# One layer on one Trainium2 core: in the mixer's step list, the query projection moves from third place to just ahead of the query convolution

## The chip, the cores and the metric

The kernel runs on one core of one Trainium2 chip. The metric is device time in microseconds, from three runs of the kernel before: a median of 1311.32 us, the lowest 1310.68, the highest 1312.76. One execution more was taken with the hardware profiler, and all the rows below come from it. In this document PE is the matrix engine (TensorE), DVE is VectorE, ACT is ScalarE, POOL is GpSimd and SP is the engine that issues the loads. Each of them works through its own instructions in their order.

## What is computed

One layer works on 512 latent tokens and 256 context tokens of width 1024, in fp32: a feed-forward block, a mixer, another feed-forward block and a norm. Only the beginning of the mixer matters here. There, one input projection yields the following, each from its own columns of `w_in`:

```python
proj = h_all @ w_in
hg_q, hg_i, hg_g, hg_f_fwd, hg_f_bwd, ml_q, ml_k, ml_v, ml_o, ml_gates = jnp.split(proj, splits, axis=-1)
qk = jax.nn.silu(short_conv(jnp.concatenate([ml_q, ml_k], axis=-1), conv_w, conv_b, n_ctx)).astype(f32)
gates = ml_gates.astype(f32) + ml_gate_b.astype(f32)
i_fwd, f_fwd, i_bwd, f_bwd = jnp.split(gates, 4, axis=-1)
logf_dir = jax.nn.log_sigmoid(jnp.concatenate([f_fwd, seg_reverse(f_bwd, n_ctx)], axis=0))
```

`short_conv` is a depthwise convolution, 3x3 over the latent grid and 3 taps over the context. From the gates come running sums and running maxima over the tokens, in both directions; they weigh the keys and values of the mLSTM heads.

## The kernel before

All products are made from operands that are split into a high and a low part, so each product takes three matmuls (high by high, high by low, low by high). For a weight tile, `load_w` (line 274) has SP load 128x1024 numbers (512 KB) into a buffer `wraw`, ACT round them into `whi`, and DVE subtract to get `wlo`. There are **two** buffers `wraw`, so a load waits until the DVE subtraction that last read its buffer is over. `whi` and `wlo` have three buffers each. The mixer's own pool has eight buffers named `d6`, which hold many things in turn, and eight PSUM banks: five named `mm` and three named `aux`.

The mixer is a list of steps, `MIXER` (line 37). Each name is a step and a number; the loop at line 1181 calls them in that order, and a scheduler orders the instructions of each engine when the kernel is built, mostly along that list, by its own estimates of time. So the order on each engine is fixed before the kernel runs. The steps that matter:

- `iv1`: a half of the HGRN2 values, 144 matmuls of 256 columns into three banks (`proj_v`).
- `ck0`, `ck1`: the convolution of the two halves of the keys (`ml_conv_ctx`, `ml_conv_lat`): POOL clears a padded `d6` buffer, ACT copies the projection into it, DVE does 3 taps on 256 columns and 9 taps on 512, ACT a sigmoid, DVE a product.
- `mq0`: the query projection, two weight tiles, 48 matmuls of 512 columns. Its first tile's two parts lie in `d6` buffers (`spare`, line 1154), the second's in `whi` and `wlo`.
- `vals0`: a half of the mLSTM values together with the gates (`proj_vg`, line 715), 144 matmuls of 272 columns: 256 of values and 16 of gates. The two weight tiles lie in four `d6` buffers of 272 columns. Their last 16 columns come from another small load (`in_wg`) and are split by themselves, two small instructions each on ACT and DVE. Each of the six token tiles' gates is copied by ACT to a buffer.
- `rows0`: the gate rows (`ml_rows`, line 901): PE turns the gates over (6 transposes); then a chain of some 30 instructions on ACT and DVE, on 36 or 4 rows by 768: absolute value, exponential, logarithm, running sums and maxima, exponentials.
- `cols0` (`ml_cols`, line 980): PE turns the results of the gate rows over (10 transposes). It waits for `rows0`.
- `cq1`, `cq0`: the convolution of the two halves of the queries. `iv0`, `vals1`: the other halves of the values, 144 matmuls each. `pair0` and the rest of the list: the heads themselves. `pair0` begins on PE with 6 transposes of the keys.

Of the kernel before, what the change touches and what calls it, by code (L numbers as in the profile page):

```python
# [23 lines left out]
for _n, _w in (("nw", 32), ("bmod", 72), ("gb", 1), ("cw", 36), ("cbias", 4), ("hgw", 4), ("mlw", 4)):  # L24
# [9 lines left out]

MIXER = ("iv1 ck0 mq0 vals0 ck1 rows0 cq1 cols0 iv0 vals1 cq0 pair0 pair0 pair0 pair1 prep0 prep0 fin4 scan0 "
         "pair1 scan0 prep1 state0 pair1 prep1 state0 prep2 scan1 scan1 state1 prep2 state1 prep3 scan2 fin0 "
         "fin5 scan2 prep3 gate0 fin1 state2 gate5 state2 scan3 gate1 scan3 gate7 state3 fin2 gate2 gate6 "
         "state3 gate4 fin3 gate3").split()  # L40
# [58 lines left out]
class Builder:  # L99
# [1043 lines left out]
    def mixer(self, st, start):  # L1143
# [36 lines left out]
        going = {}  # L1180
        for x in MIXER:
            if x not in going:
# [392 lines left out]
```

## Time and profile before

| what | us |
|---|---|
| median of three runs | 1311.32 |
| the profiled execution, its own time | 1312.59 |
| span of the profiled execution, first to last instruction | 1310.8 |
| PE busy in the span | 1286.0 (98%) |
| DVE busy | 1012.4 (77%) |
| ACT busy | 578.0 (44%) |
| POOL busy | 56.5 (4%) |
| the chain that ended last: share on PE | 94% |

The mixer's list begins at about 584 us of the span and ends at about 905 us. The views used below are the page of the profile (its chain that ended last), the busy time of the engines by stretches, the timelines of single engines (start, duration, engine, line, operation, destination and sources, shape, count; in square brackets the idle time ahead and what ended it), and the summary of the tile `wraw`. Line 56 stands for all instructions, since a helper records them, so rows are told apart by their tiles and shapes. The clock column is the TensorE clock that was granted, as a share of 2.4 GHz; 0.50 is the lower level of 1.2 GHz.

### The profile page before, as it was taken

What the parts mean: (1) busy time and instruction counts of PE and PEld (TensorE: products, weight loads), DVE (VectorE), ACT (ScalarE), POOL (GpSimd) and SP (SyncE); (2) the same over time, 40 slices, a digit from 0 to 9 for tenths busy, and PEclk for the clock granted to TensorE, in tenths of its full rate; (3) what the DMA queues carried; (4) which work ended last, traced back from release to release, by engine and by line L of the source; (5) the groups of instructions that cost most, each with busy time, mean ns of one, the idle gap of its engine ahead of it and who ended that gap; (6) DMA issues with size and microseconds to landing.
All of it is one profiled execution on the core that took longest, in us unless ns stands there. A gap on an engine that the chain in (4) does not pass through costs nothing.

```text
span 1310.8 us, 20560 instructions
## 1 busy us (share of the span) xinstructions
PE 1286.0 (98%) x8210; PEld 1179.8 (90%) x8210; DVE 1012.4 (77%) x1620; ACT 578.0 (44%) x992; POOL 56.5 (4%) x81
## 2 busy tenths in 40 slices
PE   8999999999999999999989999999999999999997
PEld 4689999999998888999978798889998999999996
DVE  6995778777789888767676867986588788888766
ACT  5553444444442222383457343444473444444434
POOL 2000000000000000110100000000000000000001
PEclk8999999999999999999989999999999999999998
DMA  9224443344686866413041101114233222233301
GB/s 347 106 93 151 140 146 125 133 140 145 214 289 228 271 209 195 145 47 117 3 145 49 65 34 49 65 50 175 83 107 136 97 97 97 102 108 104 106 17 65
DMA packets 48803, 163.60 MB, mean 125 GB/s; under 512 B 5554, under 2 KB 10034, under 8 KB 48708
## 3 DMA queue, kind: packets, MB, share of 16 engines
q1 hardware_dynamic: 46308, 150.50, 33.4%
q0 software_dynamic: 2400, 11.80, 2.8%
q8 instruction: 64, 1.05, 0.3%
q14 instruction: 31, 0.25, 0.1%
HBM read 149.39 MB, written 12.89 MB: 124 GB/s over the span
## 4 chain that ended last, share of the span: by engine, by line
PE 94%; DVE 2%; ACT 2%; issue 1%; POOL 0%; DMA 0%; POOLq 0%; DVEq 0%
PE mm L56 72%; PE aux L56 21%; DVE mod_scr L56 1%; ACT xh L56 1%; DVE x L56 0%; ACT nm_y L56 0%; ACT x L56 0%; DVE wlo L56 0%; ACT nm_t L56 0%; ACT whi L56 0%; DVE xl L56 0%; POOL rms_acc L56 0%; DVE s L56 0%; DVE nm_x L56 0%; DMA four<-in_cc 0%
## 5 line engine op out<-in xcount | busy, mean ns | idle before, releaser
L56 PE MATMUL mm<-xh,whi 128*128 128x256 f32 (+2 forms) x1072 | 345.7, 323 | 1.2 <-ACT xh L56 1.2
L56 PE MATMUL mm<-xh,wlo 128*128 128x256 f32 (+2 forms) x1072 | 342.4, 320 | 0.8 <-DVE wlo L56 0.8
L56 PE MATMUL mm<-xl,whi 128*128 128x256 f32 (+2 forms) x1000 | 323.4, 324 | 2.9 <-DVE xl L56 2.9
L56 PEld LDWEIGHTS mm<-xh,whi 128*128 128x128 f32 x1072 | 203.3, 190 | 14.3 <-ACT xh L56 1.9
L56 PEld LDWEIGHTS mm<-xh,wlo 128*128 128x128 f32 x1072 | 203.4, 190 | 10.8 <-DVE wlo L56 1.0
L56 PE MATMUL mm<-six,whi 128*128 128x384 f32 (+1 forms) x752 | 209.3, 359 | 0.0
L56 PEld LDWEIGHTS mm<-xl,whi 128*128 128x128 f32 x1000 | 189.8, 190 | 14.7 <-DVE xl L56 4.3
L56 ACT ACTIVATE whi<-wraw 128x1024 fp32r<-128x1024 f32 x100 | 105.9, 1062 | 170.4 <-PE aux L56 91.5
L56 PEld LDWEIGHTS mm<-six,whi 128*128 128x128 f32 x752 | 135.7, 188 | 10.0
L56 PE MATMUL mm<-six,wlo 128*128 128x384 f32 (+1 forms) x376 | 134.4, 357 | 0.0
L56 DVE TENSOR_TENSOR wlo<-wraw,whi 128x1024 fp32r<-128x1024 f32 x100 | 121.7, 1219 | 10.5 <-ACT whi L56 10.4
L56 DVE CUSTOM_DVE_ANT_0 mod_scr<-wm,cb 128x1024 bf16<-128x1024 f32 x84 | 105.4, 1255 | 2.8 <-DMA wm<-in_w_mod 2.6
L56 PEld LDWEIGHTS mm<-six,wlo 128*128 128x128 f32 x376 | 70.6, 188 | 6.5
L56 DVE SCALAR_TENSOR_TENSOR x<-mm,mod_l,x 128x256 f32<-128x256 f32 (+1 forms) x88 | 51.9, 601 | 18.3 <-PE mm L56 17.5
L56 DVE TENSOR_TENSOR wlo<-four,whi 128x1024 fp32r<-128x1024 f32 x37 | 45.3, 1225 | 26.7 <-ACT whi L56 26.7
L56 PE MATMUL aux<-ah,w2hi 128*128 128x512 f32 x160 | 64.0, 400 | 0.0
L56 ACT ACTIVATE whi<-four 128x1024 fp32r<-128x1024 f32 x37 | 39.2, 1061 | 56.1 <-PE mm L56 46.1
L56 PE MATMUL aux<-al,w2hi 128*128 128x512 f32 x160 | 63.1, 394 | 0.0
L56 DVE SCALAR_TENSOR_TENSOR x<-aux,mod_l,x 128x512 f32<-128x512 f32 x80 | 58.9, 745 | 5.2 <-PE aux L56 5.2
L56 PE MATMUL aux<-ah,w2lo 128*128 128x512 f32 x160 | 62.4, 390 | 0.0
L56 PE MATMUL mm<-tl,whi 128*128 128x256 f32 x216 | 61.0, 283 | 0.0
L56 PE MATMUL aux<-six,whi 128*128 128x256 f32 x320 | 59.0, 282 | 0.0
(336 smaller groups left out, 2553.8 us busy)
## 6 DMA issues: line engine op xcount, KB each, us to landing
wraw<-in_f1w SPq DMA_DIRECT2D x62, 512.0 KB, 3.9
wm<-in_w_mod SPq DMA_DIRECT2D x58, 512.0 KB, 4.0
wraw<-in_f2w SPq DMA_DIRECT2D x44, 512.0 KB, 3.4
wraw<-in_wi SPq DMA_DIRECT2D x32, 512.0 KB, 3.3
w2raw<-in_f2w SPq DMA_DIRECT2D x22, 512.0 KB, 4.2
four<-h SPq DMA_DIRECT2D x22, 384.0 KB, 4.7
h<-x POOLq DMA_DIRECT2D x18, 384.0 KB, 3.0
wraw<-in_wo SPq DMA_DIRECT2D x8, 512.0 KB, 4.0
```

The source lines that it names most:

```text
L56: r = f(*a, **kw)
```

## The change

One word moves in the list:

```diff
-MIXER = ("iv1 ck0 mq0 vals0 ck1 rows0 cq1 cols0 iv0 vals1 cq0 pair0 pair0 pair0 pair1 prep0 prep0 fin4 scan0 "
+MIXER = ("iv1 ck0 vals0 ck1 rows0 mq0 cq1 cols0 iv0 vals1 cq0 pair0 pair0 pair0 pair1 prep0 prep0 fin4 scan0 "
```

The scheduler then puts the instructions of all engines in another order from this place to the third head. What is done stays the same. Three places follow. The numbers behind a name tell buffers of one name apart.

**DVE, from the first split for the moved projection to the small splits of the gate columns** (`w2_5547` is the first key half's latent convolution, `w2_5809` and `w2_5818` or `w2_5747` and `w2_5756` the second's). Before; `d6_5562` and `wlo_5593` are the low parts of `mq0`, `d6_5630` and `d6_5638` those of `vals0`, `wlo_5932` of `iv0`:

```order
L56 TENSOR_TENSOR d6_5562<-wraw_5560,d6_5561 128x1024
L56 TENSOR_SCALAR w2_5547<-d6_5544,cst_110 128x512
L56 SCALAR_TENSOR_TENSOR w2_5547<-d6_5544,cst_110,w2_5547 128x512
L56 TENSOR_TENSOR wlo_5593<-wraw_5591,whi_5592 128x1024
L56 SCALAR_TENSOR_TENSOR w2_5547<-d6_5544,cst_110,w2_5547 128x512 x3
L56 TENSOR_TENSOR d6_5630<-wraw_5628,d6_5629 128x4x256
L56 SCALAR_TENSOR_TENSOR w2_5547<-d6_5544,cst_110,w2_5547 128x512 x4
L56 TENSOR_TENSOR d6_5638<-wraw_5636,d6_5637 128x4x256
L56 SCALAR_TENSOR_TENSOR d6_5315<-w2_5547,w2_5557 128x512
L56 TENSOR_TENSOR wlo_5932<-wraw_5930,whi_5931 128x1024
L56 TENSOR_TENSOR d6_5630<-w2_5626,d6_5629 128x4x16
L56 TENSOR_TENSOR d6_5638<-w2_5626,d6_5637 128x4x16
```

Now; `d6_5576` is a low part of `vals0`, `wlo_5864` the second one of `mq0`:

```order
L56 TENSOR_TENSOR d6_5576<-wraw_5574,d6_5575 128x4x256
L56 SCALAR_TENSOR_TENSOR w2_5547<-d6_5544,cst_110,w2_5547 128x512 x6
L56 TENSOR_TENSOR wlo_5864<-wraw_5862,whi_5863 128x1024
L56 SCALAR_TENSOR_TENSOR w2_5547<-d6_5544,cst_110,w2_5547 128x512
L56 SCALAR_TENSOR_TENSOR d6_5315<-w2_5547,w2_5557 128x512
L56 TENSOR_SCALAR w2_5747<-d6_5744,cst_110 128x256
L56 TENSOR_SCALAR w2_5756<-d6_5753,cst_110 128x512
L56 SCALAR_TENSOR_TENSOR w2_5747<-d6_5744,cst_110,w2_5747 128x256
L56 SCALAR_TENSOR_TENSOR w2_5756<-d6_5753,cst_110,w2_5756 128x512
L56 SCALAR_TENSOR_TENSOR w2_5747<-d6_5744,cst_110,w2_5747 128x256
L56 SCALAR_TENSOR_TENSOR w2_5756<-d6_5753,cst_110,w2_5756 128x512
L56 TENSOR_TENSOR d6_5568<-w2_5564,d6_5567 128x4x16
```

The small split now stands behind the first six instructions of the second key half.

**ACT, around the small splits of the gate columns** (`w2_5557` is the sigmoid of the first key half, `d6_5753` the padded buffer of the second, `whi_5931` the high part for `iv0`). Before:

```order
L56 COPY hv_5314<-mm_5375 128x2x256
L56 ACTIVATE w2_5557<-w2_5547 128x512
L56 ACTIVATE whi_5931<-wraw_5930 128x1024
L56 ACTIVATE d6_5629<-w2_5626 128x4x16
L56 ACTIVATE d6_5637<-w2_5626 128x4x16
```

Now, from the high part of the second tile of `mq0`:

```order
L56 ACTIVATE whi_5863<-wraw_5862 128x1024
L56 COPY hv_5314<-mm_5375 128x2x256
L56 ACTIVATE w2_5557<-w2_5547 128x512
L56 COPY d6_5753<-mm_5139 128x8x64
L56 ACTIVATE whi_5931<-wraw_5930 128x1024
L56 ACTIVATE d6_5567<-w2_5564 128x4x16
L56 ACTIVATE d6_5575<-w2_5564 128x4x16
```

A high part for `iv0` stands ahead of the small splits in both. Its load, number 5930, is the fifth of the stretch in both; before, it took the buffer of `wraw_5628` (`vals0`), now it takes that of `wraw_5862` (`mq0`), because the other buffer is held by `wraw_5831`, the first tile of `mq0`, until that is split.

**ACT, in the gate rows** (`d6_5840` and `d6_5843`, or `d6_5778` and `d6_5781`, belong to the gate rows; `d6_5893` is the padded buffer of the query convolution `cq1`; `d6_5832` is the high part of the first tile of `mq0`). Before:

```order
L56 ACTIVATE d6_5840<-d6_5839 36x768
L56 ACT_TABLE_LOAD
L56 ACTIVATE d6_5840<-d6_5840 36x768
L56 COPY d6_5893<-mm_5597 128x8x64
L56 ACT_TABLE_LOAD
L56 ACTIVATE d6_5840<-d6_5840 36x768
L56 ACTIVATE whi_6173<-wraw_6172 128x1024
```

Now, from the same instruction on:

```order
L56 ACTIVATE d6_5778<-d6_5777 36x768
L56 ACTIVATE d6_5832<-wraw_5831 128x1024
L56 ACT_TABLE_LOAD
L56 ACTIVATE d6_5778<-d6_5778 36x768
L56 ACT_TABLE_LOAD
L56 ACTIVATE d6_5778<-d6_5778 36x768
L56 ACTIVATE whi_6095<-wraw_6094 128x1024
L56 COPY d6_5893<-mm_5868 128x8x64
L56 ACT_TABLE_LOAD
L56 ACTIVATE d6_5778<-d6_5778 4x768
L56 ACTIVATE d6_5781<-d6_5778 4x768
```

A split for `mq0` now stands inside the chain, and so does the copy of the second result of `mq0` (`mm_5868`). On PE, `mq0` begins right behind the gates' six transposes, and the ten transposes of `cols0` follow after its 48 matmuls and 43 of `iv0`; before, 217 matmuls of `iv0` and `vals1` stood between the two.

## Rows read from the trace of the kernel before

**Rows 1.** The page: the chain that ended last, shares by engine.
```profile
PE 94%; DVE 2%; ACT 2%; issue 1%; POOL 0%; DMA 0%; POOLq 0%; DVEq 0%
```

**Rows 2.** Stretches: length, busy PE, PEld, DVE, ACT, POOL, clock, DMA share, GB/s.
```profile
659.00:660.00 1.00, 0.00 (x0) 0.00 (x0) 0.25 (x1) 0.97 (x2) 0.00 (x0) 0.50 0.91 297
666.00:667.00 1.00, 1.00 (x11) 1.00 (x10) 0.96 (x2) 1.00 (x5) 0.00 (x0) 1.00 0.79 172
...
672.00:905.00 233.00, 230.11 (x1493) 199.72 (x1492) 178.31 (x385) 105.00 (x240) 7.54 (x7) 1.00 0.17 59
```

**Rows 3.** Timeline of PE, 599 to 673 us.
```profile
599.98 0.40 PE L56 MATMUL mm<-xh,d 128*128 128x512 f32 x1
...
610.88 0.42 PE L56 MATMUL mm<-d,xh 128*128 128x272 f32 x2
...
628.92 0.29 PE L56 MATMUL mm<-d,xl 128*128 128x272 f32 x1
629.05 1.03 PE L56 MATMUL aux<-ident,d 128*128 128x128 f32 x6
629.83 0.36 PE L56 MATMUL mm<-whi,xh 128*128 128x256 f32 x1
...
655.82 0.28 PE L56 MATMUL mm<-whi,xh 128*128 128x256 f32 x1
660.14 2.37 PE L56 MATMUL aux<-ident,d 128*128 128x128 f32 x10 [4.04 <-issue]
...
672.35 0.82 PE L56 MATMUL aux<-ident,d 128*128 128x128 f32 x6
```

**Rows 4.** Timeline of ACT, 591 to 603 us.
```profile
591.54 0.59 ACT L56 COPY hv<-mm 128x512 f32<-128x512 f32 x1 [0.92 <-PE mm L56]
...
595.07 1.06 ACT L56 ACTIVATE d<-wraw 128x1024 fp32r<-128x1024 f32 x1 [1.99 <-DMA wraw<-in_wi]
...
600.77 0.63 ACT L56 ACTIVATE w<-w 128x512 f32<-128x512 f32 x1
...
602.26 0.38 ACT L56 ACTIVATE d<-w 128x64 fp32r<-128x64 f32 x2
```

**Rows 5.** Timeline of DVE, 594 to 608 us.
```profile
594.26 2.32 DVE L56 SCALAR_TENSOR_TENSOR w<-d,cst,w 128x512 f32<-128x512 f32 x3
596.49 1.22 DVE L56 TENSOR_TENSOR d<-wraw,d 128x1024 fp32r<-128x1024 f32 x1
...
603.71 0.35 DVE L56 TENSOR_TENSOR d<-w,d 128x64 fp32r<-128x64 f32 x2
...
606.65 1.01 DVE L56 SCALAR_TENSOR_TENSOR w<-d,cst,w 128x256 f32<-128x256 f32 x2
```

**Rows 6.** Tile `wraw`, 580 to 665 us: its loads, from issue to landing.
```profile
DMA to landing us min/median/max: 3.1/3.3/4.3
```

**Rows 7.** Timeline of ACT, the gate rows.
```profile
629.58 2.35 ACT L56 ACTIVATE d<-aux,cst 36x256 f32<-36x256 f32 x4
...
632.83 1.28 ACT L56 ACT_TABLE_LOAD   x1
634.12 0.85 ACT L56 ACTIVATE d<-d 36x768 f32<-36x768 f32 x1
...
655.76 5.15 ACT L56 ACTIVATE d<-d 4x768 f32<-4x768 f32 x6
```

**Rows 8.** Timeline of DVE, the gate rows.
```profile
635.00 0.55 DVE L56 TENSOR_SCALAR d<-d 36x768 f32<-36x768 f32 x1 [16.66 <-ACT d L56]
...
639.14 0.94 DVE L56 TENSOR_TENSOR d<-d,d 36x768 f32<-36x768 f32 x1
...
640.68 1.74 DVE L56 TENSOR_TENSOR_SCAN d<-d,d 36x768 f32<-36x768 f32 x1
...
644.95 0.73 DVE L56 SCALAR_TENSOR_TENSOR w<-d,cst,w 128x512 f32<-128x512 f32 x1
...
653.69 0.94 DVE L56 TENSOR_TENSOR d<-rows_sm,d 36x768 f32<-36x768 f32 x1
```

## The prediction

> **What bounds the kernel now.** I read the chain that ended last first: it lies on PE for 94% [rows 1]. So a change of order can win only where PE stands still or runs slowly, and loses whatever new standstill it makes. Next I looked for PE's standstills in the mixer, by stretches. From the keys' transposes at 672.35 us [rows 3] to the mixer's end, PE is busy 230.11 of 233 us [rows 2]: 2.9 us at most are to be had there. The one large standstill is ahead of it. PE's last matmul before it starts at 655.82, and the ten transposes of `cols0` start at 660.14, after 4.04 us of nothing [rows 3]. What ended it stands on ACT: six exponentials from 655.76, 5.15 us in all, 0.86 each [rows 7]; the fifth ends at 660.06, and PE begins 0.08 us later. They close the chain of the gate rows, which began at 629.58.
>
> The standstill has a second price. The granted clock is at 0.50 by 659 and back at 1.00 by 666 [rows 2]: it fell while PE stood still and came back some 5.5 us after PE had resumed. At full clock a transpose takes 0.13 us (six in 629.05 to 629.83) and a 256-column matmul 0.120 (217 in 629.83 to 655.82 and its own 0.12) [rows 3]. The 10 transposes and 71 matmuls from 660.14 to 672.35 should take 1.3 + 8.5 = 9.8 us and took 12.2: 2.4 us more. With 0.3 us of small change, the stretch from 599.98 (first `mq0` matmul) to 672.35 takes 72.4 us for 65.7 us of work: 10.9 for `mq0`, 18.0 for `vals0`, 0.9 for the gates' transposes, 26.0, 1.3 and 8.5 [rows 3]. So **6.7 us are lost there before**. The work of this stretch is the same after the change, so I work out what is lost in it then.
>
> **The change, part by part.** First, **PE comes to `vals0` at 599.98**, where `mq0` began. Are its operands there? Until then both kernels do the same, so times of before hold. The last of its operands are the small splits of the gate columns, and I follow both engines that make them.
>
> DVE: ACT's copy of `hv` at 591.54 is now ahead of the copy into the first key half's padded buffer, which then runs from 592.0 (0.48 later) to 592.6, taking the duration of the same shape [rows 4]. Taps on 512 columns take 0.78 us each (three in 2.32), a split 1.22 with the next starting 1.14 later [rows 5]. From 592.6: the first two taps (0.55 as in the same form at [rows 8], rounded with its lead to 0.6, and 0.78), to 594.0; the split of `d6_5576` to 595.1; six taps to 599.8; the split `wlo_5864` to 600.9; the ninth tap to 601.7; ACT's sigmoid, 0.63 [rows 4], to 602.3; the closing product, 0.7, to 603.0. Then the six instructions of the second key half that now stand ahead of the small split: three on 256 columns at about 0.5 [rows 5] and three on 512 that alternate with them at 0.6 to 0.7, 3.3 us, to 606.3. The small split takes 0.2 [rows 5]: **606.4 or so**.
>
> ACT: the load of `wraw_5862` goes out when its buffer is free, at 595.1, and lands 3.3 us later (3.1 to 4.3) [rows 6]; one such load was waited for until 595.07 [rows 4]. Its high part is ready at 599.5, in time for DVE. The load of `wraw_5930` needs the same buffer, so it goes out at 600.95 behind `wlo_5864` and lands at 604.25; its high part takes 1.06, and the small ones 0.2 each [rows 4]: 605.5. All ACT instructions behind `whi_5931` wait with it, the small splits among them. PE's first two matmuls need only high parts and run then; the third needs DVE's. So PE works steadily from 606.4 with two matmuls (0.25) done: it loses 606.4 - 0.25 - 599.98 = 6.2 us. Such a standstill is longer than the one at 656, and I charge the same 2.4 us of slow clock: **8.6 us**. No row shows this wait. Bounds: without the clock's fall 6.2; with both loads at 4.3 us 9.6.
>
> Second, **from the end of `vals0` to `cols0`**. Count from L, the start of its last matmul (628.92 before). ACT's four copies begin at L + 0.66 and its table load, behind the absolute value, at L + 3.91 [rows 3, 7]. Now the split `d6_5832` stands there, 1.06 us [rows 4]: ready at A = L + 4.95. PE is through with the gates' transposes at L + 0.9 and needs `d6_5832` for its next matmul, so it **stands still for 4 us**; I expect the slow clock again. `mq0` then ends at A + 10.9 + 2.4 = A + 13.3.
>
> The chain goes on: table load 1.28 and exponential 0.85 [rows 7], A + 2.15. The next four instructions (0.55, then of the kind of 0.94 [rows 8], with a logarithm of 0.85 behind a table load that runs beside them) take 3.3 us, A + 5.45. From the first scan at 640.68 to the end of the operation at 653.69 + 0.94 it took 13.9 us before, with five taps of `cq1` in between at 0.7 net each (one of 0.73 shown) [rows 8]; without them 10.4: A + 15.9. ACT's last exponentials need that and, ahead of them in ACT's order, a split that waits for the end of `mq0`, the copy of its result and a table load: A + 13.3 + 1.0 + 0.5 + 1.3 = A + 16.1. Both come out nearly alike, so it matters little whether the clock falls here. The fifth exponential ends 4.3 later: `cols0` starts at A + 20.3 = L + 25.2. PE's work between is 0.9 + 10.9 + 43 x 0.12 = 17.0 us. So **8.2 us are lost**, of which some 4 in the first standstill, 2 in a second just before `cols0`, and the rest to the clock. Bounds: 7.1, if the split of `d6_5832` costs the chain nothing; 9.5, if the taps cost only 0.45 each in the old chain.
>
> The ScalarE page of the Trainium skill ("ScalarE: Activation LUTs", What ACT_TABLE_LOAD costs) gives 1283 ns for a load and some 1380 ns of drain behind it. The row agrees on the first and not on the second: 632.83 + 1.28 is 634.11, and the exponential starts at 634.12 [rows 7]. By the Trainium skill's drain, the two loads that lie on the chain would add 2.8 us, and the sum below would be +12.9 instead of +10.1.
>
> Third, **behind `cols0`**: 10 transposes and 245 matmuls at full clock, 30.7 us, with all their operands there, since their splits stand tens of microseconds ahead on both engines. Then the heads. DVE comes to them with its convolutions done, which can win back at most the 2.9 us of [rows 2]; but the scheduler has put fewer weight matmuls between the heads' short dependent ones, which can cost as much. I take zero, with -2.9 and +3 for the range.
>
> Sum: 8.6 + 8.2 - 6.7 = **+10.1 us**. The profiled execution took 1312.59 us at a span of 1310.8, 1.3 above the median; a time like its own would be 1322.7, and from the median of 1311.3 I predict **1321.4 us**.
>
> **The rivals.** (a) *The clock holds through the wait at `vals0`, or the heads win back their idle time*: -2.4, -2.9 or both, 1316.1 to 1319.0. For it: the short standstills behind 672 go by at a clock of 1.00 [rows 2]. Against it: the one of 4.04 us did not. (b) *More is lost*: late loads, +1; a third slow stretch after the 2 us ahead of `cols0`, +2.4; heads with fewer fillers, +3: up to 1328. (c) *The gate rows are covered*, the other side. One mechanism, at `cols0`: the chain starts some 11 us sooner and alone on DVE, which sat idle for 16.66 us ahead of it [rows 8], and PE never waits for it: 6.7 us gone, 1304.6. It decides from the point where `cols0` comes within 17.0 us of L and `vals0` finds its operands at 600. Against it: the chain sums to 25.2 us without one tap in it. (d) *Each table load holds ACT for 1.38 us more*: two lie on the chain to the last exponentials, +2.8, 1324.2. Against it stands the start at 634.12 [rows 7]. That would be the rule of the Trainium skill's ScalarE page.
>
> **How the numbers follow.** About 0.2% (2.6 us) is what a measurement of this kernel can tell from no change. Forecast, 1319 to 1324: 0.58. (a): 0.16. (b): 0.16. (d): 0.02. (c): 0.04. That the two standstills come out so much smaller that the sum stays within 0.2%: 0.04. Low and high take in most of (a) and (b): 1315.5 to 1327.5. Faster 0.04, same 0.04, slower 0.92.
>
> **What would show it.** In the profile after: PE idle from about 600.0, its first 272-column matmul at 605.5, ended by ACT or DVE writing `d`; a clock of 0.50 in that stretch; a second standstill of 4 us between the gates' six transposes and the first 512-column matmul, near 627.5 to 631.6; ten transposes near 652; the keys' six transposes near 682.4 rather than 672.35. The prediction is wrong if PE runs on at 600, or if the 512-column matmuls follow the gates' transposes at once.

## The result, and the profile after the change

The changed kernel takes 1322.0 us (median of four runs, 1320.3 to 1322.3) and the kernel before 1311.8 (median of four, 1310.7 to 1312.8): a ratio of 1.0069, with a 95% interval of 1.0058 to 1.0081. By the two medians it is slower by 10.2 us, by the ratio by 9.1 us (the ratio is not the quotient of the two medians), and by the interval by 7.6 to 10.6 us. The profiled execution has a span of 1320.3 us, 9.5 more than before.

The chain that ended last has moved off PE by three points, against [rows 1]:

```profile
PE 91%; DVE 4%; ACT 3%; issue 1%; DMA 0%; POOL 0%; POOLq 0%; DVEq 0%; ACTq 0%
```

PE's timeline of the changed kernel, the places that answer to [rows 3]:

```profile
600.34 0.28 PE L56 MATMUL mm<-whi,xl 128*128 128x256 f32 x1
605.81 1.46 PE L56 MATMUL mm<-d,xh 128*128 128x272 f32 x3 [5.19 <-ACT d L56]
607.07 0.43 PE L56 MATMUL mm<-d,xl 128*128 128x272 f32 x1
...
627.01 0.29 PE L56 MATMUL mm<-d,xl 128*128 128x272 f32 x1
627.14 1.03 PE L56 MATMUL aux<-ident,d 128*128 128x128 f32 x6
631.89 0.50 PE L56 MATMUL mm<-xh,d 128*128 128x512 f32 x1 [3.72 <-ACT d L56]
...
644.50 0.28 PE L56 MATMUL mm<-whi,xh 128*128 128x256 f32 x1
...
652.79 2.05 PE L56 MATMUL aux<-ident,d 128*128 128x128 f32 x10 [2.98 <-ACT d L56]
...
684.90 0.82 PE L56 MATMUL aux<-ident,d 128*128 128x128 f32 x6
```

There are three stops where the kernel before had one: 5.19 us ahead of `vals0`, 3.72 us between the gates' six transposes and `mq0`, 2.98 us ahead of the ten transposes of `cols0`. The row of each names ACT as what ended it. Behind the first, PE's third weight load, at 606.67, still waited 0.36 us for DVE's small split (606.40, below).

The busy time by stretches shows the slow clock behind each stop (the columns are those of [rows 2], the clock is the third from the right), and in its last row the rest of the mixer:

```profile
606.00:607.00 1.00, 0.96 (x3) 0.64 (x4) 1.00 (x4) 0.33 (x1) 0.00 (x0) 0.50 0.00 0
611.00:612.00 1.00, 1.00 (x6) 1.00 (x6) 0.93 (x3) 0.00 (x0) 0.00 (x0) 0.50 0.47 188
612.00:613.00 1.00, 1.00 (x9) 1.00 (x8) 0.70 (x1) 0.71 (x3) 0.18 (x1) 0.89 0.00 0
631.00:632.00 1.00, 0.11 (x1) 0.11 (x2) 0.13 (x1) 0.98 (x2) 0.00 (x0) 1.00 0.00 0
633.00:634.00 1.00, 1.00 (x4) 0.71 (x3) 0.10 (x1) 0.98 (x2) 0.00 (x0) 0.50 0.00 0
636.00:637.00 1.00, 1.00 (x5) 0.78 (x4) 0.90 (x2) 0.44 (x1) 0.00 (x0) 0.94 0.00 0
652.00:653.00 1.00, 0.21 (x2) 0.22 (x3) 0.96 (x2) 0.98 (x2) 0.00 (x0) 1.00 0.62 250
654.00:655.00 1.00, 1.00 (x6) 1.00 (x6) 0.96 (x2) 0.62 (x3) 0.00 (x0) 0.50 0.96 393
657.00:658.00 1.00, 1.00 (x10) 1.00 (x10) 1.00 (x3) 0.00 (x0) 0.00 (x0) 1.00 0.00 0
...
682.00:915.00 233.00, 232.52 (x1515) 202.52 (x1514) 176.36 (x383) 104.61 (x240) 8.44 (x7) 1.00 0.19 60
```

In the rest of the mixer PE idles 0.5 us of 233, where it idled 2.9 before [rows 2].

What the stops wait for stands on ACT, DVE and SP. ACT of the changed kernel (rows of this kind in [rows 4, 7]):

```profile
604.55 1.06 ACT L56 ACTIVATE whi<-wraw 128x1024 fp32r<-128x1024 f32 x1 [1.16 <-DMA wraw<-in_wi]
605.52 0.39 ACT L56 ACTIVATE d<-w 128x64 fp32r<-128x64 f32 x2
...
630.80 1.04 ACT L56 ACTIVATE d<-wraw 128x1024 fp32r<-128x1024 f32 x1
631.86 1.28 ACT L56 ACT_TABLE_LOAD   x1
633.15 0.84 ACT L56 ACTIVATE d<-d 36x768 f32<-36x768 f32 x1
...
648.39 5.21 ACT L56 ACTIVATE d<-d 4x768 f32<-4x768 f32 x6 [0.94 <-DVE d L56]
```

DVE, with the small splits of the gate columns (as in [rows 5]) and the operation that ends its part of the gate rows and lets ACT's exponentials begin at 648.39:

```profile
604.28 2.20 DVE L56 SCALAR_TENSOR_TENSOR w<-d,cst,w 128x256 f32<-128x256 f32 x4
606.40 0.35 DVE L56 TENSOR_TENSOR d<-w,d 128x64 fp32r<-128x64 f32 x2
...
647.40 0.95 DVE L56 TENSOR_TENSOR d<-rows_sm,d 36x768 f32<-36x768 f32 x1
```

SP's queue, with the issue of the loads (591.90: three weight loads in 9.79 us, the third of which waits for its buffer; 601.86: the gate columns):

```profile
591.90 9.79 SPq L279 DMA_DIRECT2D wraw<-in_wi  x3
601.86 0.33 SPq L719 DMA_DIRECT2D w<-in_wg  x1
```

This last row is one that the prediction did not look for. The gate columns, 64 KB, are not even asked for until 601.86, so no split of them could have run at 600, however ACT and DVE were ordered.

### The profile page after: what moved, and what is told of

Same layout as the page of the kernel before. It is cut to its first block, busy times and chain, and to the rows that moved or that the text cites. A ratio compares the mean times of both kernels' runs of the same rounds, so it can differ in the third digit from the quotient of the medians.

```text
span 1320.3 us, 20564 instructions
## 1 busy us (share of the span) xinstructions
PE 1291.0 (98%) x8210; PEld 1183.5 (90%) x8210; DVE 1013.2 (77%) x1620; ACT 578.3 (44%) x993; POOL 57.4 (4%) x81
## 4 chain that ended last, share of the span: by engine, by line
PE 91%; DVE 4%; ACT 3%; issue 1%; DMA 0%; POOL 0%; POOLq 0%; DVEq 0%; ACTq 0%
PE mm L56 70%; PE aux L56 21%; DVE d L56 1%; ACT d L56 1%; DVE mod_scr L56 1%; ACT xh L56 0%; DVE x L56 0%; DVE w L56 0%; ACT whi L56 0%; ACT nm_y L56 0%; DVE wlo L56 0%; ACT x L56 0%; DVE xl L56 0%; DMA wraw<-in_wi 0%; ACT nm_t L56 0%
## 5 line engine op out<-in xcount | busy, mean ns | idle before, releaser
L56 PEld LDWEIGHTS mm<-xh,whi 128*128 128x128 f32 x1072 | 203.6, 190 | 13.8 <-ACT xh L56 1.7
L56 PEld LDWEIGHTS mm<-xl,whi 128*128 128x128 f32 x1000 | 190.1, 190 | 14.8 <-DVE xl L56 4.3
L56 DVE TENSOR_TENSOR wlo<-wraw,whi 128x1024 fp32r<-128x1024 f32 x100 | 121.8, 1219 | 16.2 <-ACT whi L56 16.1
```

What stands on the lines that cost most here:

```text
L56: r = f(*a, **kw)
```

## The experiments

The runs were made in four groups, each beside its own runs of the kernel before (medians 1312.8, 1312.8, 1313.3 and 1312.8). Differences to that kernel of the same group are compared, with the changed kernel at +10.2. In the changed kernel's own group the kernel before came out at 1311.8, 1.0 to 1.5 us lower, so a gain on the changed kernel that is taken from these differences is uncertain by about 1 us; lengths of stops and stretches come from the traces. Each kernel's list is that of the changed kernel from `cq0` on, unless the diff says otherwise.

| run | us | against before | ratio, 95% interval |
|---|---|---|---|
| e1, `vals0` ahead of `ck0` | 1313.2 | +0.3 | 0.9993 to 1.0010 |
| e2, wait filled with matmuls | 1319.7 | +6.9 | 1.0040 to 1.0065 |
| e3, `iv0` ahead of `mq0` | 1316.0 | +3.2 | 1.0014 to 1.0032 |
| e4, e1 and e3 together | 1308.2 | -4.6 | 0.9948 to 0.9976 |
| e5, gate columns loaded early | 1313.2 | +0.4 | 0.9991 to 1.0009 |
| e6, `mq0`'s splits early | 1318.7 | +5.9 | 1.0032 to 1.0057 |
| e7, before, `cols0` later | 1310.8 | -2.0 | 0.9978 to 0.9996 |
| e8, splits and `vals0` early, `iv0` ahead of `cols0` | 1305.7 | -7.0 | 0.9936 to 0.9961 |
| e9, before, `qi` later | 1309.8 | -3.5 | 0.9962 to 0.9984 |
| e10, e8 with the keys early | 1315.1 | +1.8 | 1.0005 to 1.0023 |
| e11, e4 with `qi` later | 1305.2 | -7.6 | 0.9926 to 0.9953 |

### The first stop: e1 and e5

The list of e1, against that of the changed kernel:

```diff
-iv1 ck0 vals0 ck1 rows0 mq0 cq1 cols0 iv0 vals1
+iv1 vals0 ck0 ck1 rows0 mq0 cq1 cols0 iv0 vals1
```

> The changed kernel with `vals0` ahead of `ck0` in the list; nothing else. Loads, splits and small gate splits of `vals0` then stand ahead of both key convolutions on SP, ACT and DVE. Theory: the whole first loss of the changed kernel (PE still from 600.6 to 605.8, then slow clock to 612; 26.7 us for 18.2 us of `vals0`) is the late operands, so 8.5 us go and the second loss stays as it is: 1322.0 - 8.5 = 1313.5 us. Rival: the clock falls there for a reason other than the stop, then only 5.3 us go: 1316.7. Second rival: the convolutions, now behind `vals0` on DVE, push the gate rows back (DVE idled 16.3 us ahead of them, so this needs more than that): above 1316.

It comes out 9.9 us below the changed kernel by the differences in the table, and 8.9 us by the spans of the two profiled executions. In its trace the first 272-column matmul follows the last of `iv1` after 0.12 us, at 599.17, and the six transposes come 18.2 us later. The other two stops are still there, as the summary of PE's waits from 580 to 920 us shows (in all, times, longest):

```profile
PE mm L56 <- ACT d L56: 3.7, 1, 3.7
PE aux L56 <- ACT d L56: 2.9, 1, 2.9
```

So the two losses are separate, and the first is worth about what was reckoned, 8.5 us. But e1 moves the load, both kinds of splits and the convolutions at once. e5 moves one load of 64 KB and nothing else in the code:

```diff
+def gl(_):                       # first in the list
+    self.graw = mp.tile([P, KT, 16], F32, name="w2", bufs=self.W2)
+    nc.sync.dma_start(out=self.graw, in_=T["wg"])
...
-graw = self.mp.tile([P, KT, 16], F32, name="w2", bufs=self.W2)
-nc.sync.dma_start(out=graw, in_=self.T["wg"])
+graw = self.graw
```

> The changed kernel with one load moved: the gate columns (64 KB), issued at 601.86 us in the changed kernel behind a weight load that waits for a buffer, are now loaded at the head of the list; the list itself is that of the changed kernel, both key convolutions stand as they did. Theory, formed after the first runs: this load is the root of the late small splits, and the scheduler, which knows the load to be late, put them behind the convolutions for that reason. Then PE runs on at 600.5 as with `vals0` ahead of `ck0`: 8.5 us less than the changed kernel, 1313.5. Rival, the two mechanisms of the prediction alone: the taps on DVE and the high part of `wraw_5930` on ACT still hold the small splits, 1320 to 1322.

It takes the same time as e1. The summary of the tensor `in_wg` gives its issue, 18 us sooner than at 601.86:

```profile
L1161 SPq DMA_DIRECT2D w<-in_wg x1: 337/337/337, 583.8 to 583.8; - x1
```

The order of ACT and DVE follows from it: with the columns there, the scheduler puts the small splits beside the large ones on ACT (592.49 and 593.60) and among the first taps of `ck0` on DVE, all by itself. DVE:

```profile
593.10 0.22 DVE L56 TENSOR_TENSOR d<-w,d 128x64 fp32r<-128x64 f32 x1
...
595.70 0.22 DVE L56 TENSOR_TENSOR d<-w,d 128x64 fp32r<-128x64 f32 x1
```

PE runs on into `vals0` at 599.97, 0.12 us behind the last matmul of `iv1`. The late load is the root. The taps on DVE and the high part of `wraw_5930` on ACT, by which the prediction reckoned 606.4 and 605.5, are what then stood ahead of the splits.

### The price of the clock: e2

e2 is the changed kernel with 20 more matmuls ahead of `vals0`:

```diff
+fill = self.aux.tile([P, 512], F32, name="aux")
+for _ in range(20):
+    nc.tensor.matmul(fill, lhsT=self.xh[0][:, :P], rhs=self.xh[0][:, :512],
+                     start=True, stop=True)
 for t in range(6):               # the matmuls of vals0
```

> The changed kernel with 20 more matmuls of 512 columns (4.5 us at full clock) that nobody reads, put on PE between the end of `iv1` and `vals0`, where it stood still for 5.2 us; the operands of `vals0` come as late as before. It measures the price of the slow clock apart from the stop. Theory: PE busy there keeps the clock at 1.00, `vals0` then takes 18.2 us and not 21.3, and the time falls by 2.4 to 3.1 us, to 1319.2. Rival: the clock falls whatever PE does there: 1322.0, or more if the added matmuls outlast the wait.

It does 4.7 us more work on PE and is 3.3 us faster than the changed kernel. PE's timeline, and then the stretches:

```profile
600.13 4.72 PE L56 MATMUL aux<-xh 128*128 128x512 f32 x20
605.70 1.05 PE L56 MATMUL mm<-d,xh 128*128 128x272 f32 x6 [0.84 <-ACT d L56]
```

```profile
606.00:612.00 6.00, 6.00 (x49) 6.00 (x48) 5.86 (x11) 0.55 (x3) 0.00 (x0) 1.00 0.28 89
...
628.00:629.00 1.00, 0.26 (x1) 0.26 (x2) 0.28 (x1) 0.98 (x2) 0.00 (x0) 0.50 0.00 0
630.00:634.00 4.00, 4.00 (x10) 3.05 (x10) 2.96 (x4) 2.96 (x3) 0.00 (x0) 0.50 0.44 133
```

`vals0` still cannot start before 605.70, but the clock stays at 1.00, and it takes 18.3 us (to 623.99) instead of 21.3. From the end of `iv1` to the gates' transposes it takes 23.9 us instead of 26.7, so 2.8 us are won. So of the 8.5 us that the first stop cost, some 2.8 were clock. The next stop, of 3.72 us, which nothing fills, has its slow clock as ever; here it begins before PE resumes at 628.74, and `mq0` takes 13.8 us (12.6 in the changed kernel). The third stop is shorter for that (1.99 us), since `cols0` comes at almost the same time, 26.0 us after the last matmul of `vals0`. The clock stays at 1.00 behind it, and another 1.4 us are won between `cols0` and the keys' transposes (30.8 us, 649.85 to 680.61).

### The second loss: e3, e4 and e6

The list of e3, against that of the changed kernel:

```diff
-rows0 mq0 cq1 cols0 iv0 vals1
+rows0 iv0 mq0 cq1 cols0 vals1
```

> The changed kernel with `iv0` between `rows0` and `mq0` in the list. `vals0` still waits (its gate columns are loaded behind a load that waits for a buffer), so the first 8.5 us stay. Theory: with 144 matmuls of `iv0` (17.3 us) behind the gates' transposes, the split for `mq0` is covered, and with `mq0` (10.9) PE has 29.1 us of work from the last matmul of `vals0` to `cols0`, whose operands came 25.8 us after it. Both stops of this stretch (3.7 and 3.0 us) and both slow stretches go, 10.2 us in all: 1311.8. Rival: the end of the gate rows moves back with the work put ahead (copies of `iv0` on ACT stand ahead of the last exponentials), and a stop before `cols0` stays: 1314 to 1318.

The list of e4, against that of the changed kernel:

```diff
-iv1 ck0 vals0 ck1 rows0 mq0 cq1 cols0 iv0 vals1
+iv1 vals0 ck0 ck1 rows0 iv0 mq0 cols0 cq1 vals1
```

> The changed kernel with `vals0` ahead of `ck0`, `iv0` between `rows0` and `mq0`, and `cols0` ahead of `cq1`: both cures together. Theory: the two losses are separate and add up, so 8.5 + 10.2 us go: 1303.3, about 8 us below the kernel before, which loses 6.7 us in this stretch. Rival: they share a cause or new stops take their place (`iv0` then needs its weights 8.5 us sooner): 1306 to 1312.

In e3 both stops of the second loss are gone: the ten transposes start at 655.98, 0.24 us behind the last matmul of `mq0`. Yet it wins 7.0 us and not 10.2. Its first stop is 0.5 us longer (5.68), and its heads are slower: from the keys' transposes (674.34) to the first use of `wo3h` (a part of the mixer's output weights, used where its list ends; 905.3) it takes 231.0 us, the changed kernel 228.5 (684.9 to 913.4). The same holds for e4: no stop is left, 65.6 us from the first matmul of `vals0` (600.65) to the keys' transposes (666.23) for the 65.7 us of work, but 231.1 us for the heads. Within what the runs can tell the losses add up: 9.9 + 7.0 = 16.9 us by the table against 14.8 for both together, and 8.9 + 7.4 = 16.3 against 15.7 by the spans. In both e3 and e4 the 2.6 us that the changed kernel won at the heads are paid back. Both times lie in the ranges of the rivals, but not for the rivals' reasons: no stop ahead of `cols0` stayed in e3, and in e4 none took the place of the old ones ahead of the keys' transposes. That the heads would be slow again stood in neither expectation.

e6 takes only the loads and splits for `mq0` out of the way (`proj` then takes the finished parts):

```diff
+def mw(_):
+    box["w"] = [self.load_w(self.T["wi"][W_MQ + q], None if q else spare) for q in range(2)]
...
-ck1 rows0 mq0
+ck1 mw0 rows0 mq0
```

> The changed kernel with the loads and splits of the weights of `mq0` written ahead of `rows0`; its matmuls stay behind it. The first stop of the second loss (3.7 us between the gates' transposes and `mq0`) must go if the split behind the absolute value on ACT makes it. Theory: the gate rows set `cols0`, and the split out of their way shortens them by its 1.06 us only, so `cols0` comes 24.7 us after the last matmul of `vals0` (25.8 before); PE has 0.9 + 10.9 + 76 x 0.12 = 20.9 us of work, since the scheduler now puts 76 matmuls of `iv0` ahead of `cols0`; a stop of 3.8 us and some 1.5 of slow clock remain where 10.2 us were lost: 1317. Rival: `cols0` hangs on the end of `mq0` (a copy of its result stands on ACT ahead of the last exponentials), which comes 5.6 us sooner; then no stop stays and the time is 1311.8.

`mq0` now starts at 627.31, 0.78 us behind the first transpose of the gates: the first stop was the split behind the absolute value and nothing else. The gain is 4.3 us of 10.2, since the second stop grows (PE's waits, 580 to 920 us; the first row is the stop ahead of `vals0`):

```profile
PE mm L56 <- ACT d L56: 5.4, 1, 5.4
PE aux L56 <- ACT d L56: 5.2, 1, 5.2
```

`cols0` comes 26.4 us after the last matmul of `vals0`, not sooner than the 25.8 of the changed kernel, although `mq0` ends 5.6 us sooner, counted likewise. The rival falls: the gate rows set `cols0`, and `mq0` does not. The forecast of 24.7 was 1.7 too low, since a weight split (1.19 us) and the first tap of `cq1` (0.55) had come into the gate rows on DVE:

```profile
643.25 1.19 DVE L56 TENSOR_TENSOR wlo<-wraw,whi 128x1024 fp32r<-128x1024 f32 x1
...
647.03 0.55 DVE L56 TENSOR_SCALAR w<-d,cst 128x512 f32<-128x512 f32 x1
```

### Cover for the old stop: e7

e7 is the kernel before with its ten transposes later:

```diff
-rows0 cq1 cols0 iv0 vals1
+rows0 cq1 iv0 vals1 cols0
```

> The kernel before with `cols0` behind `iv0` and `vals1` in the list: 288 matmuls (34.5 us) instead of 217 stand between the gates' transposes and the ten of `cols0`, whose operands come 31.1 us after. Theory: the stop of 4.04 us and its slow clock, 6.4 us, go; what hangs on `cols0` (the scaled keys, the weights of the pairs) then comes later at the heads: 1306.4 if that is hidden, against 1312.8 for the kernel before. Rival: the heads give it back, since `cols0` stands right ahead of the keys' transposes instead of 8.5 us ahead: 1309 to 1313.

The stop of 4.04 us is gone, and only 2.0 us are won. PE, then DVE:

```profile
657.90 0.58 PE L56 MATMUL mm<-wlo,xh 128*128 128x256 f32 x1 [2.05 <-DVE wlo L56]
```

```profile
655.16 0.94 DVE L56 TENSOR_TENSOR d<-d,d 36x768 f32<-36x768 f32 x1
656.03 0.68 DVE L56 SCALAR_TENSOR_TENSOR d<-w,w 128x512 f32<-128x512 f32 x1
656.63 2.35 DVE L56 TENSOR_TENSOR wlo<-wraw,whi 128x1024 fp32r<-128x1024 f32 x2
```

The added cover is the last matmuls of `vals1`, and the split of their weights stands on DVE behind the gate rows. The stop came back as a wait for that split, with a slow clock of its own to 661. Neither theory had this; the rival's number held for a reason that it did not name.

### The heads: e9

In the kernel before, DVE makes the two products `qi` between the first scaled keys and the others:

```profile
673.60 0.29 DVE L56 TENSOR_TENSOR ks<-d,cA 128x128 f32<-128x128 f32 x1 [1.66 <-ACT d L56]
673.81 2.44 DVE L56 TENSOR_TENSOR qi<-d,d 64x1024 f32<-64x1024 f32 x2
676.27 0.50 DVE L56 TENSOR_TENSOR ks<-d,cA 128x128 f32<-128x128 f32 x2
```

e9 is the kernel before with these four lines behind the loop:

```diff
-for h in range(2):               # ahead of the loop over ks
-    r = slice(64 * h, 64 * h + 64)
-    self.tt(qi[r, h], mq[r]..., IW[r, :, NC_:], ALU.mult)
 yield
 ...                              # the loop over ks
+for h in range(2):
+    r = slice(64 * h, 64 * h + 64)
+    self.tt(qi[r, h], mq[r]..., IW[r, :, NC_:], ALU.mult)
 yield
```

> The kernel before with one thing moved: the two products `qi` (2.4 us on DVE, made in the first step of a head pair) are written behind the loop that makes the scaled keys `ks`, where they are first needed. It asks where the 2.6 us went that the heads of the changed kernel won (228.5 us from the keys' transposes to the first use of `wo3h`, 231.1 before). Theory: in the kernel before `qi` stands on DVE between the first scaled keys and the others, and PE waits 1.7 us for `ks` because of that; without it this stretch takes 229.4, and the time falls by 1.7 us, from 1312.8 to 1311.1. Rival: the scaled keys wait for something else (the copies of the transposes on ACT): no change.

It wins 3.5 us (by the interval 2.1 to 5.0), more than the wait of 1.7. PE no longer waits for `ks` from 580 to 920 us; the heads take 228.9 us (672.55 to 901.4) instead of 231.1, and the span is 2.9 shorter. The scheduler does not put both products behind all keys: one of 1.21 us follows the first two keys (674.22) and the other the next two (676.68). In the changed kernel both stand ahead of the keys' transposes (684.90):

```profile
677.75 2.47 DVE L56 TENSOR_TENSOR qi<-d,d 64x1024 f32<-64x1024 f32 x2
```

So in the kernel before the two products right behind the first key cost 2.3 us, and that fits most of what the changed kernel won there; the changed kernel with `qi` put back between the keys was not run. In e3, whose heads are slow, `qi` stands between the keys again (679.14, behind the first key at 678.94). Where the time beyond these 2.3 us was won, if it was, stays open.

### Combinations: e8, e10 and e11

The list of e8, against that of the changed kernel, with `mw0` as in e6:

```diff
-iv1 ck0 vals0 ck1 rows0 mq0 cq1 cols0 iv0 vals1
+iv1 vals0 ck0 ck1 mw0 rows0 mq0 cq1 iv0 cols0 vals1
```

> `vals0` ahead of `ck0`; the weights of `mq0` loaded and split ahead of `rows0`; `iv0` between `mq0` and `cols0`, so that 144 matmuls stand behind `mq0`. Theory: no stop is left between 600 and the keys' transposes, as with `iv0` ahead of `mq0` (1308.2), and since the query convolutions come sooner on DVE the two instructions of 2.4 us (`qi`) no longer stand between the scaled keys there: the 1.6 us of PE's wait at the heads and about 1 us more go, 1305.6. Rival: the query convolution on DVE runs into the gate rows or the heads wait all the same: 1308 or more.

The time is as expected and 7.0 us below the kernel before, but not for the reason given: `qi` does run earlier (660.78), and PE still waits 1.7 us for `ks`. The copies of the keys' transposes stand on ACT behind a weight split that waits for its load:

```profile
667.92 1.06 ACT L56 ACTIVATE whi<-wraw 128x1024 fp32r<-128x1024 f32 x1 [3.99 <-DMA wraw<-in_wi]
668.88 0.84 ACT L56 COPY d<-aux 128x512 f32<-128x512 f32 x2
```

The heads take 230.3 us. Most of the gain is the stretch without a stop.

The list of e10, against that of e8:

```diff
-iv0 cols0 vals1 cq0 pair0 pair0 pair0
+iv0 cols0 cq0 pair0 vals1 pair0 pair0
```

> The last combination (`vals0` ahead of `ck0`, weights of `mq0` split early, `iv0` ahead of `cols0`) with the query convolution `cq0` and the first step of the first head pair, which has the keys' transposes and their copies on ACT, moved ahead of `vals1`. There ACT's copies of the transposes waited behind a weight split that waited 4.0 us for its load, and PE 1.7 us for `ks`. Theory: the copies now stand ahead of that split, the wait goes, and the time falls by 1.7 us, from 1305.7 to 1304.0. Rival: the heads start no sooner, since their second step still stands behind `vals1`, and the weights behind the copies come late instead: 1305.7 or more.

It comes out 8.8 us above e8. The keys' transposes now follow those of `cols0` and wait until ACT has copied the results of the latter (`cA`) out of their `aux` banks, as PE's timeline shows:

```profile
652.14 0.87 PE L56 MATMUL aux<-ident,d 128*128 128x128 f32 x6 [3.13 <-ACT cA L56]
```

That is 3.1 us and a slow clock; the rest was lost in the heads, where PE has new stops of 0.4 to 1.5 us, and was not followed up.

e11 is e4 with the move of `qi` from e9.

> Two gains put together: `vals0` ahead of `ck0`, `iv0` between `rows0` and `mq0`, `cols0` ahead of `cq1` (1308.2 us, all stops of this stretch gone, but 231.1 us from the keys' transposes to `wo3h`), and the products `qi` written behind the scaled keys. Theory: the 231.1 us fall to 228.8, as they did in the kernel before without that wait, so 1308.2 - 2.3 = 1305.9. Rival: here the copies of the keys' transposes on ACT come late for another reason (a weight split ahead of them), and the wait stays: 1308.

It is the fastest, 7.6 us below the kernel before; its interval overlaps that of e8. The wait did not go: in its profile PE waits 1.6 us for `ks` as in e4, and the heads take 230.4 us. There the second copy of the keys stands on ACT behind a sigmoid that waits for the convolution `cq0`, as the rival had it in kind, and on DVE the first keys stand behind the last product of `cq0`, though their copy was ready at 669.8:

```profile
672.06 0.69 DVE L56 SCALAR_TENSOR_TENSOR d<-w,w 128x512 f32<-128x512 f32 x1
672.66 0.49 DVE L56 TENSOR_TENSOR ks<-d,cA 128x128 f32<-128x128 f32 x2
```

So the time of the theory came without its mechanism. The profiled execution was also the slowest of the five (1308.5 us, the others 1304.7 to 1305.3), so where the other four won their 3 us on e4 is not shown.

## Why the prediction was right

**The total** was 1321.4 and the measurement is 1322.0: +10.1 forecast, +10.2 found. That the two lie so close is partly luck: the terms from `vals0` to the keys' transposes came out 2.0 us larger than forecast, the heads 2.6 us smaller, and the two errors cancel. The waits behind the two large terms, 8.6 and 8.2 us, are those that the traces show, the first with a cause that the prediction had not seen.

**Operands of `vals0`.** Forecast: high parts at 605.5, small splits on DVE done at 606.4 or so; 8.6 us lost. Found: 605.81 and 606.40 to 606.75; the 18.2 us of work of `vals0` took from 600.46 (0.12 behind the start of the last matmul of `iv1`) to 627.14, 8.5 lost. The engines' orders were followed rightly. What the step lacked is the cause of that order, the load at 601.86, which e5 shows. Whoever had acted on the prediction would have moved splits or taps, where moving one load was enough. The charge of 2.4 us for the clock holds: e2 gives 2.8.

**From `vals0` to `cols0`.** Forecast: a first stop of 4 us, a second of 2, `cols0` 25.2 us after the last matmul. Found: 3.72, 2.98 and 25.8. So 8.8 us were lost where 8.2 stood. The prediction had left open whether the gate rows (A + 15.9) or `mq0` (A + 16.1) set the end. It was the gate rows: with A found at 631.84, DVE ends its part at A + 16.5 (648.35), while ACT is through with the copy behind `mq0` and its table load at 647.44 and then waits 0.94 us for DVE. e6 confirms it.

**Behind `cols0`.** Here the step failed. It took 30.7 us "at full clock"; found are 32.1 (652.79 to 684.90), because the second stop drew its own slow clock. The prediction had counted that only in rival (b). With the 0.6 of the term before, the keys' transposes came 12.1 us later than before, counted from the end of `iv1` in each, and not 10.1.

**The heads** were taken at zero, with -2.9 as a bound; they won 2.6, nearly the whole bound. The prediction named the source, 2.9 us of idle time [rows 2], and the means, convolutions done earlier on DVE. e9 points to the instruction: `qi`, which in the changed kernel is made at 677.75, ahead of the keys' transposes.

**The rivals.** (a) had the heads right and the clock wrong: it fell at all three stops. (b) had the third slow stretch. (c) fell with the three stops. (d), the drain of 1.38 us that the Trainium skill's page "ScalarE: Activation LUTs" (What ACT_TABLE_LOAD costs) puts behind a table load, fell on the same evidence as before: the load at 631.86 lasts 1.28 us, and the exponential starts at 633.15, 0.01 us later.

The sum as found is 8.5 + 8.8 + 1.4 - 6.7 - 2.6 = +9.4 us, against 9.5 between the two spans.

## What to carry to other kernels

Before a step is moved ahead, list every load that it needs and where each stands in its queue: a 64 KB load behind one that waited for a buffer cost 8.5 us here, and moving that load alone in the code won them all back, since the orders of ACT and DVE followed it. A step put right behind a chain's start can steal from that chain on the engines that both use, so put work there whose operands are ready, and count the cover up to the chain's end. A stop removed by later work must be followed to that work's own operands (e7) and buffers (e10).

## What the runs showed of the hardware

Stops shorter than the 4.04 us of the kernel before are also followed by a stretch at the granted clock of 0.50, the level of 1.2 GHz. Behind the stop of 3.72 us it shows from 632 to 636, and behind that of 2.98 us from 653 to 656; in both PE had resumed before the clock fell, so it is the work behind a stop that pays: 1.7 us on `mq0` (12.6 us instead of 10.9) and 1.4 behind `cols0`. Behind a stop of the same 3.72 us in e2 the clock was down at 628, before PE resumed at 628.74, and `mq0` took 13.8 us: so two stops of one length need not cost the same behind them. In e7 a stop of 2.05 us drew a slow stretch from about 658 to 661, and in e5 one of 2.12 us from about 645 to 649. The stop of 1.99 us in e2, that of 0.84 there and the waits of up to 1.7 us at the heads passed at 1.00. These rows are too few to say at what length the clock falls. Matmuls that nobody reads, put into the longest stop, kept the clock up and made the kernel faster by 3.3 us.
